# Attention stage of a two-layer encoder: new-key copy behind the exponentials, high x parts on GpSimd, and weight casts behind the x casts

## The chip, the cores and the metric

The kernel runs on one core of one Trainium2 chip. The metric is the device time of one execution in microseconds (us). Engines are named as the profile names them: PE (TensorE, matrix products; PEld is its weight load), DVE (VectorE), ACT (ScalarE), POOL (GpSimd), SP (SyncE, which only issues DMAs here).

## The reference, cut to what matters

Two layers of an encoder process 640 rows of width 1024: 512 rows of one new stream and 16 rows of each of 8 running streams. Layer 0 is feed-forward, then an S5 state space beside stick-breaking attention, then feed-forward. Layer 1 is feed-forward, Mamba-2, feed-forward. Each part ends in a layer norm of (ALPHA * x + part).

```python
def swiglu(x, w_gate, w_up, w_down):
    return (jax.nn.silu(x @ w_gate) * (x @ w_up)) @ w_down

def sb_block(q_blk, q_pos, k, v):                       # stick-breaking attention
    z = jnp.einsum('bqhd,bkhd->bhqk', q_blk, k) * (SB_HEAD_DIM ** -0.5)
    mask = k_pos[None, :] < q_pos[:, None]
    sp = jnp.where(mask, jax.nn.softplus(z), 0.0)
    suffix = lax.cumsum(sp, axis=3, reverse=True) - sp
    w = jnp.where(mask, jnp.exp(jax.nn.log_sigmoid(z) - suffix), 0.0)
    return jnp.einsum('bhqk,bkhd->bqhd', w, v)

# mixer of layer 0
g = jax.nn.gelu(ys + d_skip * u)                        # ys: S5 output
s5_out = g * jax.nn.sigmoid(g @ w_glu + b_glu)
out = concatenate([s5_out, sb_out], axis=-1) @ w_out    # w_out: 8 blocks of 128 rows
```

## The kernel before, in words

**Products in three parts.** Each fp32 operand is split in a high part, a cast to PE's reduced fp32 format (`hi`, mostly on ACT, line 95), and a low part, the difference (`lo`, DVE, line 96). A product is three matmuls: high with high, low with high, high with low. x lies transposed in `xhi` and `xlo`, 8 blocks of 128 channels by 640 rows; the rows are five tiles t = 0 to 4 of 128. A weight block is loaded by SP into one of four `raw` tiles, and split by `load_w` into one of six `w` tiles.

**Phases.** ffn0, mix0, ffn1, ffn2, mix1, ffn3 follow each other. Within a phase a list scheduler sets each engine's order, by what it takes to be ready; `tc.issue_after(i)` puts what is traced under it behind instruction i, on the engine of i alone. It sets an order, not a wait.

**Entry of an ffn.** While the layer norm of the phase before ends, `layer_norm` leaves a closure `transposes` for each row tile t: 8 transposes on PE, and a split of their PSUM banks into `xhi` and `xlo`. Those of t = 3 and 4 run within the ffn's first products: gate and up of weight blocks f = 0 and 1 on rows 0 to 255 first, then on rows 256 to 639, which need tiles 2, 3 and 4. After them come the gate products of blocks 2 and 3 (lines 278 to 286), then `down` for blocks 0 and 1, and then pairs of blocks in a form with fewer products (`operands`, `matrix`), of which `operands` for `w_up` of f = 2 is the first: its loads go through `raw`, and one of its casts is of a single 128x512 piece into a tile of its own.

**The attention stage** (lines 914 to 1404) is written out by hand: a loop over 16 units s = (p, u), p being one of four pairs of heads, u one of four pieces of work (u = 3 is the running streams). At its end the order in which the program was traced is fixed on PE, ACT and DVE (`in_order`); POOL and SP are left to the scheduler. An iteration s holds, in this order:
- `turn(s)` transposes the weights on PE into a pair of PSUM banks z, an ACT copy (line 1361) takes them out, and `product(s)` multiplies by the values on PE.
- `begin(s + 2)` makes the scores of a later unit in z, and `soft(s + 2)` runs three ACT functions on them.
- `sums(s + 2)` on DVE adds, scans and subtracts (lines 1256, 1263, 1265), reading the same z; `expo` is then ACT's exponential of that.
- For u = 1 the idle columns of z also take a transpose of the new keys; ACT's copy of it, line 1201 into `kk`, is the first of two steps that turn the keys around (`new_keys`).

Between these, `fill` places matmuls of other work on PE: query and key projections of later pairs, the sigmoid gate of the S5 output (`glu_groups`) and the first half of the output projection (`out_groups`). Its side work waits in two lists of jobs, for ACT and for DVE; `slot(engine, us)` takes ready jobs from a list until their summed costs reach `us`. The jobs are weight splits (lines 1086, 1089), x splits (`split_x`, lines 1123, 1124), sigmoids (three ACT functions on `gs`, line 83) and evictions. Blocks 0 to 3 of `w_out` are split in the loop; blocks 4 to 7 are loaded by `load_w` behind it (line 1410), where the scheduler may place their casts between the fixed instructions.

Of the kernel before, what the change touches and what calls it, by code (L numbers as in the profile page):

```python
# [9 lines left out]
F32 = mybir.dt.float32  # L10
# [26 lines left out]
def kernel(ctx: ExitStack, tc: tile.TileContext, I, O, phases=PHASES):  # L37
# [123 lines left out]
    def layer_norm(t, g_bc, last):  # L161

        y = yacc[:, t, :]
        st = small.tile([128, 2, 6], F32, name="st")
        mv = small.tile([128, 2], F32, name="mv")
        rs = small.tile([128, 1], F32, name="rs")
        for j in range(2):
            nc.vector.bn_stats(st[:, j, :], y[:, j * 512:j * 512 + 512])  # L168
        nc.vector.bn_aggr(mv, st)
        nc.vector.tensor_scalar_add(rs, mv[:, 1:2], LN_EPS / ALPHA ** 2)  # L170
        state["pow"] = nc.gpsimd.tensor_tensor(rs, rs, mhalf, op=ALU.pow).ins
        if t < NT - 1 and not last:
# [7 lines left out]
            nc.gpsimd.tensor_tensor(y[:, hi], y[:, hi], g_bc[1][:, hi], op=ALU.add)  # L180
        else:
            nc.vector.scalar_tensor_tensor(y, y, mv[:, 0:1], g_bc[0], op0=ALU.subtract, op1=ALU.mult)  # L182
            for c in [slice(0, 512), slice(512, 1024)] if last and t == NT - 1 else [slice(0, 1024)]:
                state["ln"] = nc.vector.scalar_tensor_tensor(y[:, c], y[:, c], rs, g_bc[1][:, c],  # L184
                                                             op0=ALU.mult, op1=ALU.add).ins
                if last:
                    nc.sync.dma_start(O["y"][t * 128:t * 128 + 128, c], y[:, c])
        if last:
            return
        xh, xl = xt["hi"], xt["lo"]  # L190

        def transposes():
            for j in range(2):
                pt = bank_b().rearrange("p (k c) -> p k c", c=128)
                for k in range(4):
                    nc.tensor.transpose(pt[:, k, :], y[:, (4 * j + k) * 128:(4 * j + k) * 128 + 128], ident)
                split(xh[:, 4 * j:4 * j + 4, t * 128:t * 128 + 128],
                      xl[:, 4 * j:4 * j + 4, t * 128:t * 128 + 128], pt)

        pend.append(transposes)  # L200

# [10 lines left out]
    def ffn(i, ph, last, side=None):  # L212
# [4 lines left out]
        with ExitStack() as st:  # L217
# [58 lines left out]
            first = {}  # L276
            g_row = lambda: wk.tile([128, T], F32, name="s", bufs=2)
            for r in range(2):
                w = load_w(I["w_gate"][i, 2 + r])
                first[r] = g_row()  # L280
                for c in range(2):
                    p = bank_a()[:, :Q]
# [102 lines left out]
            def pair(f, before=None):  # L385
# [26 lines left out]
                for n, take in (("w_gate", gate), ("w_up", up)):  # L412
# [2 lines left out]
                        continue  # L415
                    if n == "w_up" and before is not None:
                        down(before)
                    with tc.issue_after(state["acc0"]) if f == 2 else ExitStack():
                        A = operands(I[n][i, f], I[n][i, f + 1])
                    if n == "w_up":  # L420
                        for r in range(2):
# [307 lines left out]
    def mixer0(ph, last):  # L729
# [184 lines left out]
        with ExitStack() as st:  # L914
# [61 lines left out]
                    self.done = True  # L976
                    self.give()

            todo = {"act": [], "dve": []}
            groups = []  # L980

            def later(engine, cost, give, *needs):
# [3 lines left out]

            def slot(engine, us):

                while us > 0:
                    todo[engine] = sorted((j for j in todo[engine] if not j.done), key=lambda j: not j.frees)  # L990
                    j = next((j for j in todo[engine] if j.ready()), None)
                    if j is None:
                        return
                    j.run()
                    us -= j.cost
# [124 lines left out]

            def split_x(k, src, o, L, needs):

                a = later("act", 0.1 + 0.001 * L, lambda: nc.scalar.copy(xh[:, k, o:o + L], src[:, o:o + L]), *needs)
# [50 lines left out]
            def out_groups():  # L1174
                for t in range(NT):
                    for j in range(2):
                        def operands(t=t, j=j):
                            for k in range(4):
                                wo[k] = ws["o", k][:, 0], ws["o", k][:, 1]
                            return bank_a(), three(x_cols(range(4), 128 * t, 128), [w_j(wo[k], j) for k in range(4)])  # L1180

                        def then(ps, t=t, j=j):
                            def give():
# [171 lines left out]
            for s, (p, u) in enumerate(units):  # L1355
# [14 lines left out]
                    streams_back(p)  # L1370
                if s + 2 < len(units):
                    soft(s + 2)
                if u == 2:
                    V.tensor_copy(qk[p, "q"][:, 0:512], po[p])
                slot("dve", 3.8)
                if u == 3:
                    streams_out(p)
                    if p < 3:
# [3 lines left out]
                if u == 0:  # L1382
                    kr[p].run()
                slot("act", 1.2)
                fill(FILL[1])
                if (p, u) == (3, 2):
                    split_x(7, qk[3, "q"], 0, TP, [made[3, n, h] for n in "qk" for h in range(2)])
            while groups:
# [1 line left out]
                    slot("act", 1)  # L1390
                    slot("dve", 1)
                fill(1)
            while todo["act"] or todo["dve"]:
# [13 lines left out]
        with ExitStack() as st:  # L1407
            ctx_p.close()
            open_banks()
            for k in range(4, 8):  # L1410
                wo[k] = load_w(I["m0_out"][k])
            gb = pool("m0_gb", 1, st, reuse_waits="tile")
            g_bc = [gb.tile([128, D], F32, name=f"gb{n}") for n in range(2)]
# [561 lines left out]
```

## Time and profile before

| what | value |
|---|---|
| device time, median of 3 runs | 2573.09 us (2572.42 to 2573.87) |
| the profiled execution | 2573.02 us; its span 2571.3 us |
| PE busy, PEld busy | 2511.2 us (98%), 2297.1 us (89%) |
| DVE, ACT, POOL busy | 2017.1 us, 1225.1 us, 287.3 us |
| mean granted clock of PE | 0.992 |
| attention stage | about 572 to 736 us of the span |
| start of ffn1, ffn2, ffn3 | about 764, 1195 and 2119 us |

A timeline row has the start in us, the duration in us, the engine, the line, the operation, the tiles it writes and reads with shapes, the number of instructions merged, and in brackets the idle time of the engine before it and what ended that. In a table by stretch each engine has its busy time, then come PEclk (the share of full speed granted to PE) and the DMA share. In a group row, what stands behind the first bar is the summed time and the mean duration in ns.

### The profile page before, as it was taken

Reading aid. Unit: us, or ns where it says so; the run is one execution under the profiler, and the core shown is the slowest. Engines: PE = TensorE matmul, PEld = TensorE weight load, DVE = VectorE, ACT = ScalarE, POOL = GpSimd, SP = SyncE. Lnnn points to the kernel's source line nnn. Section 1 sums busy time; section 2 is a strip of 40 time slices with the busy share of each in tenths; the row PEclk is TensorE's granted clock in tenths of the full one; section 3 lists DMA queues with packets and bytes.
Section 4 is the critical chain, followed back from the end, with each engine's and each line's share of the span. In section 5 each row is a group of like instructions: output and inputs, shape, how many; then the busy total and the mean of one; then the engine's idle time right before and its main releaser. Section 6 shows DMA issues by size and latency. Waiting matters only on the chain. (4 is left out here: it accounts for less than half of the span.)

```text
span 2571.3 us, 40672 instructions
## 1 busy us (share of the span) xinstructions
PE 2511.2 (98%) x15577; PEld 2297.1 (89%) x15577; DVE 2017.1 (78%) x3685; ACT 1225.1 (48%) x2329; POOL 287.3 (11%) x412
## 2 busy tenths in 40 slices
PE   8999999999899999999999999999999999999998
PEld 8999999878678999998999999889989878999997
DVE  7788877666768888887888887778686798876768
ACT  4443444336743555553455554566565443443332
POOL 0000002110030000003000002311111150000001
PEclk9999999999999999999999999999999999999999
DMA  5332334443311334443144434356564722443442
GB/s 183 107 97 86 107 115 153 150 159 101 96 53 55 107 96 110 119 126 105 53 111 114 116 106 132 114 184 193 159 203 141 238 72 80 161 150 110 143 138 95
DMA packets 174835, 317.44 MB, mean 123 GB/s; under 512 B 20480, under 2 KB 91776, under 8 KB 174128
## 3 DMA queue, kind: packets, MB, share of 16 engines
q1 hardware_dynamic: 164816, 293.83, 35.7%
q0 software_dynamic: 9824, 21.01, 4.0%
q8 instruction: 122, 2.00, 0.3%
q14 instruction: 73, 0.60, 0.1%
HBM read 259.56 MB, written 40.54 MB: 117 GB/s over the span
## 5 line engine op out<-in xcount | busy, mean ns | idle before, releaser
L96 DVE TENSOR_TENSOR w<-raw,w 128x512 fp32r<-128x512 f32 (+1 forms) x601 | 525.8, 899 | 84.7 <-ACT w L95 83.6
L95 ACT CAST w<-raw 128x512 fp32r<-128x512 f32 (+1 forms) x601 | 442.3, 776 | 289.7 <-PE bank L134 106.9
L356 PE MATMUL bank<-xhi,w 128*128 128x320 f32 x2432 | 540.0, 309 | 1.0 <-ACT mx L367 0.9
L134 PE MATMUL bank<-xhi,w 128*128 128x256 f32 (+2 forms) x2272 | 502.5, 313 | 14.5 <-ACT xhi L95 8.2
L134 PE MATMUL bank<-w,h 128*128 128x512 f32 x1872 | 435.1, 390 | 0.0
L356 PE MATMUL bank<-T,w 128*128 128x320 f32 x2736 | 426.3, 309 | 0.8 <-DVE s L393 0.4
L134 PEld LDWEIGHTS bank<-w,h 128*128 128x128 f32 x1872 | 349.2, 188 | 72.5 <-DVE h L96 1.0
L356 PEld LDWEIGHTS bank<-xhi,w 128*128 128x128 f32 x2432 | 407.4, 188 | 5.0 <-ACT mx L367 1.8
L356 PEld LDWEIGHTS bank<-T,w 128*128 128x128 f32 x2736 | 406.4, 188 | 2.8 <-DVE s L393 1.2
L134 PEld LDWEIGHTS bank<-xhi,w 128*128 128x128 f32 x2272 | 382.2, 190 | 26.1 <-ACT xhi L95 9.5
L356 PE MATMUL bank<-xlo,w 128*128 128x320 f32 x1216 | 375.1, 308 | 0.0
L134 PE MATMUL bank<-xlo,w 128*128 128x256 f32 (+2 forms) x1136 | 353.8, 312 | 5.8 <-DVE xlo L96 5.8
L356 PEld LDWEIGHTS bank<-xlo,w 128*128 128x128 f32 x1216 | 228.0, 188 | 0.3
L134 PEld LDWEIGHTS bank<-xlo,w 128*128 128x128 f32 x1136 | 215.9, 190 | 7.7 <-DVE xlo L96 7.0
L209 DVE SCALAR_TENSOR_TENSOR yacc<-bank,yacc 128x512 f32<-128x512 f32 x160 | 109.4, 687 | 77.8 <-PE bank L134 77.2
L367 ACT COPY mx<-bank 128x320 f32<-128x320 f32 x228 | 96.4, 423 | 142.2 <-PE bank L356 141.7
L96 DVE TENSOR_TENSOR w<-sw,w 128x1024 fp32r<-128x1024 f32 x76 | 93.0, 1224 | 52.9 <-ACT w L95 52.6
L95 ACT CAST w<-sw 128x1024 fp32r<-128x1024 f32 x76 | 79.8, 1051 | 99.0 <-DVE sw L335 97.9
L500 POOL DMA_DIRECT2D yacc<-ev x56 | 48.6, 904 | 651.2 <-ACT ev L499 591.2
L134 PE MATMUL bank<-w,og 128*128 128x512 f32 x432 | 104.9, 396 | 3.0 <-DVE og L1769 2.8
L134 PEld LDWEIGHTS bank<-w,og 128*128 128x128 f32 x432 | 79.6, 188 | 21.0 <-DVE og L1769 4.6
L395 ACT ACTIVATE s<-s 128x320 f32<-128x320 f32 x108 | 50.8, 471 | 84.0 <-DVE s L393 83.8
(428 smaller groups left out, 3467.0 us busy)
## 6 DMA issues: line engine op xcount, KB each, us to landing
raw<-in_w_gate_dram SPq DMA_DIRECT2D x88, 512.0 KB, 3.8
raw<-in_w_up_dram SPq DMA_DIRECT2D x88, 512.0 KB, 4.0
raw<-in_w_down_dram SPq DMA_DIRECT2D x88, 512.0 KB, 3.6
raw<-in_m_in_dram SPq DMA_DIRECT2D x52, 512.0 KB, 4.6
yacc<-ev POOLq DMA_DIRECT2D x56, 256.0 KB, 4.3
raw<-in_m_out_dram SPq DMA_DIRECT2D x24, 512.0 KB, 4.1
csb<-cs_d SPq DMA_DIRECT2D x20, 512.0 KB, 4.9
h<-in_ssd_h_dram SPq DMA_DIRECT2D x16, 512.0 KB, 6.1
```

The source lines that it names most:

```text
L95: nc.scalar.copy(hi, src)
L96: return nc.vector.tensor_tensor(lo, src, hi.bitcast(F32), op=ALU.subtract)
L134: state["pe"] = nc.tensor.matmul(ps, a, b, start=(k == 0), stop=(k == n - 1)).ins
L209: state["acc"] = nc.vector.scalar_tensor_tensor(ya, pb, scale, ya, op0=ALU.mult, op1=ALU.add).ins
L356: nc.tensor.matmul(ps, A[p][:, a, k * 128:k * 128 + 128], B[p][b][:, k, :], start=(first and n == 0), stop=(n == 11), skip_group_check=True)
L367: nc.scalar.copy(e[n], ps)
L395: state["silu"] = nc.scalar.activation(t, ps, AF.Silu).ins
L500: nc.gpsimd.dma_start(yacc[:, t, 512 * j:512 * j + 512], e, accum_op=ALU.add)
```

## The change

Five edits:
1. **New keys.** The first copy into `kk` (line 1201) is traced right behind the three functions of `soft`, ahead of `sums`, for the three later pairs of heads.
2. **x casts on POOL.** A third list of jobs, for POOL, takes the high half of `split_x`: 20 casts, of 256, 384, 512 or 640 columns. A call of `slot` for ACT or DVE first gives out all POOL jobs that are ready. The low halves stay on DVE. DVE's slot in the loop is 4.6 instead of 3.8.
3. **Two weight splits in the kept order.** Blocks 4 and 5 of `w_out` are loaded and split by `load_w` in iterations 12 and 13, and so stand at fixed places; 6 and 7 stay behind the loop.
4. **ffn weights behind the last x casts.** `layer_norm` keeps its last ACT cast of x (`xc`). The loads of gate blocks 2 and 3, and `operands` for `w_up` of f = 2, are put behind it on ACT. It is there for ffn1, ffn2 and ffn3; ffn0 has none.
5. `out_groups` no longer writes its weights into `wo`, so that blocks 4 and 5 may be placed there earlier.

```diff
@@ layer_norm, transposes @@
-                split(xh[:, 4 * j:4 * j + 4, t * 128:t * 128 + 128],
-                      xl[:, 4 * j:4 * j + 4, t * 128:t * 128 + 128], pt)
+                state["xc"] = nc.scalar.copy(xh[:, 4 * j:4 * j + 4, t * 128:t * 128 + 128], pt).ins
+                nc.vector.tensor_tensor(xl[:, 4 * j:4 * j + 4, t * 128:t * 128 + 128], pt,
+                                        xh[:, 4 * j:4 * j + 4, t * 128:t * 128 + 128].bitcast(F32), op=ALU.subtract)
@@ ffn @@
             for r in range(2):
-                w = load_w(I["w_gate"][i, 2 + r])
+                with tc.issue_after(state["xc"]) if "xc" in state else ExitStack():
+                    w = load_w(I["w_gate"][i, 2 + r])
...
-                    with tc.issue_after(state["acc0"]) if f == 2 else ExitStack():
+                    with ExitStack() as q:
+                        if f == 2:
+                            for k in ("acc0", "xc"):
+                                if k in state:
+                                    q.enter_context(tc.issue_after(state[k]))
                         A = operands(I[n][i, f], I[n][i, f + 1])
@@ mixer0 @@
-            todo = {"act": [], "dve": []}
+            todo = {"act": [], "dve": [], "pool": []}
...
             def slot(engine, us):
 
+                if engine != "pool":
+                    slot("pool", 100)
...
-                a = later("act", 0.1 + 0.001 * L, lambda: nc.scalar.copy(xh[:, k, o:o + L], src[:, o:o + L]), *needs)
+                a = later("pool", 0.1 + 0.001 * L, lambda: nc.gpsimd.tensor_copy(xh[:, k, o:o + L], src[:, o:o + L]),
+                          *needs)
...
                 if s + 2 < len(units):
                     soft(s + 2)
+                    if units[s + 2][1] == 1:
+                        kr[units[s + 2][0]].needs[0].run()
...
-                slot("dve", 3.8)
+                slot("dve", 4.6)
...
                 slot("act", 1.2)
+                if s in (12, 13):
+                    wo[s - 8] = load_w(I["m0_out"][s - 8])
...
-            for k in range(4, 8):
+            for k in range(6, 8):
                 wo[k] = load_w(I["m0_out"][k])
```

The order of PE's instructions is the same before and after, throughout the program. What moves stands on ACT, DVE, POOL and SP.

**ACT in the attention stage**, from the copy of one unit's values on (`pvs`, unit 7) to the next copy of transposed weights (`es<-bank`, unit 8), with what each instruction waits for. Before:

```order
L1303 COPY pvs<-bank 128x256 [waits PE_49]
L1246 ACTIVATE es<-bank 128x2x384 [waits PE_49]
L83 ACTIVATE es<-es 128x2x384 [waits Activation_49] x2
L1201 COPY kk<-bank 128x128 [waits DVE_49]
L83 ACTIVATE gs<-gs 128x256
L83 ACTIVATE gs<-gs 128x256 [waits Activation_49] x2
L1361 COPY es<-bank 128x1024 [waits PE_49]
```

And with the change:

```order
L83 ACTIVATE es<-es 128x2x384 [waits Activation_49] x2
L1209 COPY kk<-bank 128x128
L83 ACTIVATE gs<-gs 128x256 [waits DVE_49]
L83 ACTIVATE gs<-gs 128x256 [waits Activation_49] x2
L83 ACTIVATE gs<-gs 128x256 [waits DVE_49]
L83 ACTIVATE gs<-gs 128x256 [waits Activation_49] x2
L1369 COPY es<-bank 128x1024 [waits PE_49]
```

The copy of the new keys waited for DVE and now has no wait of its own; a second sigmoid (three functions) now stands ahead of the copy of the weights.

**ACT at the entry of ffn1**, from the table load for silu on; `xhi<-bank` are the casts of x (the two singles are those of t = 4), `hf` the silu of a gate, `w_8068` the single piece of `operands` for f = 2. Before:

```order
L272 ACT_TABLE_LOAD
L272 ACTIVATE hf<-bank 128x256
L95 CAST xhi<-bank 128x4x128 x2
L95 CAST h<-hf 128x256
L272 ACTIVATE hf<-bank 128x256
L95 CAST w_8068<-raw 128x512
L95 CAST xhi<-bank 128x4x128
L95 CAST h<-hf 128x256
L95 CAST xhi<-bank 128x4x128
L272 ACTIVATE hf<-bank 128x384
```

And with the change:

```order
L273 ACTIVATE hf<-bank 128x256
L197 CAST xhi<-bank 128x4x128
L95 CAST h<-hf 128x256
L197 CAST xhi<-bank 128x4x128
L95 CAST w<-raw 128x512 x4
L273 ACTIVATE hf<-bank 128x384
L95 CAST w<-raw 128x512 x2
L95 CAST w_8068<-raw 128x512
L95 CAST w<-raw 128x512 x2
```

The single piece moves from ahead of the x casts of t = 4 to behind them, and the four casts of gate blocks 2 and 3 follow them too.

**DVE at the entry of ffn3**, from the last layer norm instruction on; `xlo<-bank` are the low parts of x, `w<-raw` those of weights. Before:

```order
L184 SCALAR_TENSOR_TENSOR yacc<-yacc,rs,h_21059 128x1024
L96 TENSOR_TENSOR w<-raw,w 128x512 x4
L273 TENSOR_TENSOR hf<-bank,hf 128x256
L96 TENSOR_TENSOR xlo<-bank,xhi 128x4x128
L96 TENSOR_TENSOR h<-hf,h 128x256
L96 TENSOR_TENSOR xlo<-bank,xhi 128x4x128
L1439 MEMSET xrow 128x512
L1440 MEMSET brow 128x256
L1457 TENSOR_TENSOR h_21861<-h_21861,el_21843 128x512
L1457 TENSOR_TENSOR h_21906<-h_21906,el_21843 128x512
L273 TENSOR_TENSOR hf<-bank,hf 128x256
L96 TENSOR_TENSOR xlo<-bank,xhi 128x4x128
```

And with the change:

```order
L184 SCALAR_TENSOR_TENSOR yacc<-yacc,rs,h_21059 128x1024
L1451 MEMSET xrow 128x512
L1452 MEMSET brow 128x256
L274 TENSOR_TENSOR hf<-bank,hf 128x256
L198 TENSOR_TENSOR xlo<-bank,xhi 128x4x128 x2
L96 TENSOR_TENSOR h<-hf,h 128x256
L274 TENSOR_TENSOR hf<-bank,hf 128x256
L198 TENSOR_TENSOR xlo<-bank,xhi 128x4x128
L96 TENSOR_TENSOR h<-hf,h 128x256
L198 TENSOR_TENSOR xlo<-bank,xhi 128x4x128
L96 TENSOR_TENSOR w<-raw,w 128x512 x4
```

The four low parts of weights move behind the low parts of x, and the two products of line 1457 (1469 now) go further back; at the same place SP now issues twelve small loads for `xrow` and `brow` ahead of the two loads for `operands` of f = 2, where it issued them behind.

More of the change, by code (lines that the diff above doesn't have):

```diff
@@ L1177, in operands @@
                         def operands(t=t, j=j):
-                            for k in range(4):
-                                wo[k] = ws["o", k][:, 0], ws["o", k][:, 1]
-                            return bank_a(), three(x_cols(range(4), 128 * t, 128), [w_j(wo[k], j) for k in range(4)])
+                            w = [(ws["o", k][:, 0], ws["o", k][:, 1]) for k in range(4)]
+                            return bank_a(), three(x_cols(range(4), 128 * t, 128), [w_j(v, j) for v in w])
                         def then(ps, t=t, j=j):
@@ L1392, in mixer0 @@
                 fill(1)
-            while todo["act"] or todo["dve"]:
+            while any(todo.values()):
                 slot("act", 1)
```

## The prediction

> **What bounds the kernel now.** I read the page's head first, then the table of PE's waits, then the timelines around its largest stops.
>
> ```profile
> span 2571.3 us, 40672 instructions
> PE 2511.2 (98%) x15577; PEld 2297.1 (89%) x15577; DVE 2017.1 (78%) x3685; ACT 1225.1 (48%) x2329; POOL 287.3 (11%) x412
> ...
> PE bank L1285 <- ACT es L1361: 12.9, 5, 4.9
> ...
> ACT kk L1201 <- DVE S L1265: 11.2, 3, 3.9
> ```
>
> PE is busy for 98% of the span and does the same products in the same order with the change. So a gain can come only from its 60.1 us of idle time (2571.3 - 2511.2), and from slow-clock stretches that follow a stop. A row of waits has the total, the number of waits and the longest. PE's row is its largest: attention products waiting for the copied weights (the stops at the entries of the feed-forward parts come below). The other row, from ACT's waits, says why the copy of weights is late: the new-keys copy ahead of it waits for DVE's sums.
>
> ```profile
> 624.31 1.09 PE L1285 MATMUL bank<-es,vt 128*64 128x128 f32 x16 [1.01 <-ACT es L1361]
> 662.47 1.97 PE L1285 MATMUL bank<-es,vt 128*64 128x128 f32 x16 [4.01 <-ACT es L1361]
> 673.66 0.88 PE L1285 MATMUL bank<-es,vt 128*64 128x128 f32 x12 [0.66 <-ACT es L1361]
> 683.39 1.55 PE L1285 MATMUL bank<-es,vt 128*64 128x128 f32 x12 [4.87 <-ACT es L1361]
> 700.78 1.03 PE L1275 MATMUL bank<-ident,S 128*128 128x128 f32 x8
> 706.00 1.58 PE L1285 MATMUL bank<-es,vt 128*64 128x128 f32 x16 [2.35 <-ACT es L1361]
> ```
>
> The bracket is the stop. A stop also costs clock behind it. In the table by stretch PEclk stands behind POOL's column:
>
> ```profile
> 624.30:628.00 3.70, 3.69 (x42) 3.36 (x43) 1.29 (x2) 3.46 (x6) 0.00 (x0) 1.00 0.41 109
> 662.50:666.00 3.50, 3.50 (x28) 2.88 (x29) 2.55 (x6) 3.44 (x7) 0.00 (x0) 0.57 0.22 35
> 683.40:689.00 5.60, 5.60 (x23) 3.38 (x24) 4.23 (x8) 4.21 (x7) 0.00 (x0) 0.50 0.05 19
> 706.00:710.00 4.00, 4.00 (x31) 3.27 (x32) 0.10 (x1) 0.95 (x2) 0.00 (x0) 0.57 0.00 0
> 784.20:789.00 4.80, 4.78 (x17) 4.78 (x17) 4.44 (x10) 0.76 (x2) 0.00 (x0) 0.56 0.00 0
> 2135.30:2144.00 8.70, 6.60 (x23) 6.28 (x24) 6.96 (x16) 1.51 (x3) 0.00 (x0) 0.61 0.39 135
> ```
>
> Behind the 1.01 us stop the clock stayed at 1.00; behind 2.35, 4.01 and 4.87 it was 0.50 to 0.57. PE's busy time times (1 - clock) is what a stop costs besides its length.
>
> **New keys, the copy (edit 1).** ACT around the longest of these waits:
>
> ```profile
> 654.46 1.73 ACT L83 ACTIVATE es<-es 128x768 f32<-128x768 f32 x2
> 660.04 0.27 ACT L1201 COPY kk<-bank 128x128 f32<-128x128 f32 x1 [3.85 <-DVE S L1265]
> 660.21 1.31 ACT L83 ACTIVATE gs<-gs 128x256 f32<-128x256 f32 x3
> 661.43 0.99 ACT L1361 COPY es<-bank 128x1024 f32<-128x1024 f32 x1
> 665.19 0.84 ACT L83 ACTIVATE S<-S 128x768 f32<-128x768 f32 x1
> 674.12 1.63 ACT L83 ACTIVATE gs<-gs 128x384 f32<-128x384 f32 x3
> 676.69 0.81 ACT L1246 ACTIVATE es<-bank 128x768 f32<-128x768 f32 x1 [0.20 <-PE bank L1237]
> 682.56 0.78 ACT L1361 COPY es<-bank 128x768 f32<-128x768 f32 x1
> ```
>
> *662.47.* PE was free at 662.47 - 4.01 = 658.46. With the change: exponentials end at 654.46 + 1.73 = 656.19, the key copy takes 0.27, two sigmoids (the order has a second one here) 2 x 1.31, and from the copy's start to PE it is 662.47 - 661.43 = 1.04. That is 660.1, so 1.7 remains and 2.3 is gained. A stop of 1.7 lies between one that kept the clock (1.01) and one that lost it (2.35); I take it as kept, which saves 3.50 x 0.43 = 1.5, with 0 as the other end.
>
> *683.39.* The product before it started at 673.66. The absolute value started 676.69 - 673.66 = 3.03 behind that; then come 0.81, the exponentials 1.73, one sigmoid 1.63 and 683.39 - 682.56 = 0.83: 8.03 against 9.73 before. Gain 1.7; a stop of 3.2 remains, and with it the slow clock (5.60 x 0.50 = 2.8, which I do not count).
>
> *706.00.* PE was free at 703.65. Its transposes end at 701.81, and 1.04 later the weights could be used, 0.8 ahead of need. The stop goes: 2.35, and 4.00 x 0.43 = 1.7 of clock. *624.31* goes too (1.0), as does 673.66 (0.6), since ACT is less loaded.
>
> Together 1.0 + 2.3 + 1.5 + 1.7 + 2.35 + 1.7 + 0.6 = 11.15.
>
> **Casts on POOL (edit 2), splits in the order (edits 3, 5).** Twenty casts leave ACT for POOL. Their price on POOL is in no row; the nearest are these, with the row of sixteen casts on ACT, and DVE's weight splits, first alone, then while POOL adds:
>
> ```profile
> L778 POOL COPY r8t<-r 128x256 f32<-128x256 f32 x4 | 1.8, 454 | 57.4 <-DVE zb L817 57.4
> ...
> L1482 POOL TENSOR_SCALAR cw<-cw 128x120 f32<-128x120 f32 x1 | 1.7, 1661 | 0.0
> ...
> 767.45 1.63 POOL L180 TENSOR_TENSOR yacc<-yacc,gb 128x512 f32<-128x512 f32 x1
> ...
> L1123 ACT CAST xhi<-g x16: 388/460/524, 632.1 to 703.9; 128x256 fp32r<-128x256 f32 x8, 128x384 fp32r<-128x384 f32 x8
> ...
> 1206.90 1.28 DVE L96 TENSOR_TENSOR w<-raw,w 128x512 fp32r<-128x512 f32 x2
> ...
> 766.73 2.90 DVE L96 TENSOR_TENSOR w<-raw,w 128x512 fp32r<-128x512 f32 x2
> ```
>
> ACT is rid of 16 x 0.46 = 7.4 us and of four longer ones, all beside PE except where it stood ahead of a copy (0.6, counted above). The row of sixteen covers 8 x 256 + 8 x 384 columns, the other four by the code 3 x 640 + 512: 7552. The copy gives 454 / 256 = 1.77 ns a column, 13.4 us in all; the two-input add 3.2 ns, 24 us; the tensor-scalar 13.8 ns, 104 us. I take the copy, the only row with one input and one output of this width. POOL had 11% to do, so even 24 us there costs nothing by itself; a cast costs only where DVE's low half behind it, in DVE's fixed order, delays the sums. The cover for that is about 5 us: the sums of the unit at 660 were ready when the key copy went (660.04), and their exponential ran at 665.19.
>
> On DVE, slot 4.6 instead of 3.8 puts up to 0.8 us more ahead of some sums, mostly another weight split of 0.64; and POOL's reading can stretch a split from 0.64 to 1.45 (half of 2.90), by 0.81. Bounds: 0 (all in the cover) to 8 (half of twenty such blocks on the path). I take 0.5, near the covered end, because of those 5 us. The Trainium skill's page "SBUF — State Buffer" (section "Who interferes with whom") states that a DVE instruction with two SBUF inputs contends with a GpSimd one that reads SBUF, and that the later is blocked completely; the row at 766.73 agrees in kind. By it every low half and scan that meets a cast would be late: the upper end.
>
> The casts of blocks 4 and 5 on ACT move to later iterations. I cost that at nothing: four casts of some 0.6 are spread over two iterations, and without ACT's idle time there they would be 1.2 each, ahead of one copy. Attention: 11.15 - 0.5 = 10.65.
>
> **Weights behind the x casts (edit 4), ffn1 and ffn2.**
>
> ```profile
> 783.07 0.62 ACT L95 CAST w<-raw 128x512 fp32r<-128x512 f32 x1 [3.35 <-DMA raw<-in_w_up_dram]
> ...
> 784.22 1.97 PE L134 MATMUL bank<-xhi,w 128*128 128x384 f32 x5 [4.73 <-ACT xhi L95]
> ...
> 1207.16 1.14 PE L134 MATMUL bank<-xhi,w 128*128 128x384 f32 x5 [0.24 <-ACT xhi L95]
> 1209.17 0.44 PE L134 MATMUL bank<-xlo,w 128*128 128x384 f32 x1 [0.87 <-DVE xlo L96]
> ```
>
> In ffn1 the single piece of the up weights waits 3.35 for its DMA, and the x casts of t = 4 stand behind it on ACT. In ffn2, where nothing stands ahead of them, the same stop is 0.24. So 4.73 - 0.24 = 4.5 goes, and the clock loss 4.78 x 0.44 = 2.1: 6.6. The piece then waits behind the x casts, with casts for gate blocks 2 and 3 around it; PE has over 8 us of products on rows 256 to 639 first, so I cost that at nothing, and at the 3.35 if that cover is gone. In ffn2 the two splits at 1206.90 stood ahead of the low part of x; behind it, the stop of 0.87 goes: 0.9.
>
> **ffn3.**
>
> ```profile
> 2131.25 2.48 DVE L96 TENSOR_TENSOR w<-raw,w 128x512 fp32r<-128x512 f32 x4
> 2133.66 0.41 DVE L273 TENSOR_TENSOR hf<-bank,hf 128x256 f32<-128x256 f32 x1
> ...
> 2135.32 1.14 PE L134 MATMUL bank<-xhi,w 128*128 128x384 f32 x5 [2.72 <-ACT xhi L95]
> 2135.65 0.48 DVE L1439 MEMSET xrow<- 128x512 f32 x1
> ...
> 2136.34 1.22 DVE L1457 TENSOR_TENSOR h<-h,el 128x512 f32<-128x512 f32 x2
> ...
> 2138.54 0.69 PE L134 MATMUL bank<-xlo,w 128*128 128x384 f32 x1 [2.08 <-DVE xlo L96]
> ```
>
> Four splits delay `hf` (2133.66), ACT's cast of h waits for it, and the x cast stands behind. With the change two memsets stand there: 0.48 and about half that. So `hf` ends near 2131.25 + 0.75 + 0.41 = 2132.4; ACT then has the three steps that took 2135.32 - 2134.07 = 1.25 from the end of `hf` to PE: near 2133.7. PE was free at 2135.32 - 2.72 = 2132.60, so 1.1 to 1.2 remains of 2.72. Of the second stop (2.08) I leave 0.4 for the low halves. Gain 1.5 + 1.7 = 3.2; two stops near 1 keep the clock, 6.60 x 0.39 = 2.6. Off go 0.5 for splits now late on DVE and for the loads of `operands` behind twelve small loads on SP: 5.3, with 2.7 (no clock) and 5.8 as ends.
>
> **Sum.** Attention 10.65, ffn1 6.6, ffn2 0.9, ffn3 5.3: 23.45. The profiled execution took 2573.02, 1.7 above its span and 0.07 below the median, so I use it as it is: 2573.02 - 23.45 = 2549.6, said as 2549.5.
>
> **Rivals.**
>
> *A, more clock.* The remaining stop near 683 does not lose the clock: 2.8 more, 2546.7. Against: a stop of 2.35 lost it at 706. The Trainium skill's page "TensorE: Matmul & The Clock Gate" (section "What's actually happening") says that the clock halves after an idle window of about 3.4 us that runs on freely; by that rule 3.2 may escape, and 2.35 should have. The row disagrees, so the rule only speaks for some luck with the window's phase.
>
> *B, POOL and DVE block each other.* 20 x 0.81 = 16.2, half on the path: 8 instead of 0.5, 2557. For: the row at 766.73. Against: the 5 us cover.
>
> *C, the entries pay half.* Another instruction (the silu, `hf`) becomes what the x casts wait for: half of 12.8, 2556. Against: ffn2's stop of 0.24 in the same order.
>
> *D, slower.* POOL casts go at the tensor-scalar's 13.8 ns a column. A batch of 4 x 384 + 640 = 2176 columns then takes 30 us, four casts of 256 take 14, and the later 2688 columns 37. DVE's low halves wait for them in order, ahead of sums; beyond 5 to 10 us of cover each, some 59 of these 81 us come on the path and the attention gain is lost: 2573.0 - 12.8 + 59 = 2619. It decides from about 8 ns a column, or 2 us for a cast of 256. Against: the copy's 454 ns.
>
> *E, the copy still waits* (on the bank or the new `kk` tile): attention gains some 2, 2558. Against: the order shows no wait on it.
>
> **Chances.** Forecast 0.48, A 0.22, B 0.15, C 0.08, D 0.04, E 0.03. About 0.2% (5.1 us) is what a measurement of this kernel can tell from no change; only D is slower (0.04), I leave 0.02 for a sum of half-failures within it, and 0.94 is faster. The forecast's own range, from the ends named (clock at 662, 0 to 2 on DVE, 2.6 at ffn3), is 2545.5 to 2553; to hold 8 in 10 with A and most of B and C it is 2543 to 2559.
>
> **What would show it.** Right: no wait of the key copy on DVE's sums; PE's stops on the weights' copy falling from 12.9 to about 5, nearly all in two stops of 1.7 and 3.2; clock 1.00 behind 662 and 706; POOL casts near 0.45 us for 256 columns; the stop in ffn1 near 0.24, and in ffn3 two of about 1. Wrong: DVE waiting for POOL's `xhi` ahead of sums, scans or splits that got longer, a new stop of PE at the gate products of blocks 2 and 3 or at the first products of pairs, or a clock that stays at 0.5 where the stop went.

## The result and the profile after

The changed kernel takes 2548.61 us (median of five runs, 2542.40 to 2551.85) against 2573.09 us before (five runs beside it, 2570.48 to 2573.91). The ratio is 0.9899, with a 95% interval of 0.9885 to 0.9913: 1.0% faster, 24.5 us. The forecast was 2549.5. The profiled execution took 2548.97 us.

From here on, lines of the changed kernel are its own: the copy into `kk` is L1209 (L1201 before), the copy of the weights L1369 (L1361), the product L1293 (L1285), the cast of x at a feed-forward part's entry L197 (L95), the cast on POOL L1131 (L1123 on ACT).

The page's head and two rows of PE's waits, after:

```profile
span 2547.3 us, 40681 instructions
...
PE 2501.8 (98%) x15577; PEld 2289.1 (90%) x15577; DVE 2017.0 (79%) x3685; ACT 1218.0 (48%) x2309; POOL 298.3 (12%) x432
...
PE bank L1293 <- ACT es L1369: 4.3, 2, 3.0
...
PE bank L134 <- ACT xhi L197: 1.8, 4, 1.1
```

The last of these rows, before:

```profile
PE bank L134 <- ACT xhi L95: 8.2, 5, 4.7
```

The span is 24.0 us shorter. PE's idle time fell from 60.1 to 45.5 us (2547.3 - 2501.8), its busy time by 9.4 us although its products are the same: that part is clock (the mean granted clock rose from 0.992 to 0.997). The two waits fell from 12.9 to 4.3 and from 8.2 to 1.8 us.

PE's remaining stops at the places of the change, from the timeline, and the granted clock (1.00 or 0.50, behind POOL's column) behind the first two, behind 694, where the stop of 2.35 us had been, and in ffn1:

```profile
658.75 1.09 PE L1293 MATMUL bank<-es,vt 128*64 128x128 f32 x16 [1.34 <-ACT es L1369]
675.05 1.55 PE L1293 MATMUL bank<-es,vt 128*64 128x128 f32 x12 [3.00 <-ACT es L1369]
768.13 1.14 PE L134 MATMUL bank<-xhi,w 128*128 128x384 f32 x5 [0.24 <-ACT xhi L197]
1189.11 1.14 PE L134 MATMUL bank<-xhi,w 128*128 128x384 f32 x5 [0.24 <-ACT xhi L197]
2115.45 1.14 PE L134 MATMUL bank<-xhi,w 128*128 128x384 f32 x5 [1.08 <-ACT xhi L197]
```

```profile
658.70:662.70 4.00, 3.95 (x39) 3.62 (x40) 3.40 (x8) 2.45 (x3) 0.81 (x2) 1.00 0.03 9
675.00:680.60 5.60, 5.55 (x23) 3.33 (x24) 5.17 (x9) 3.91 (x6) 1.54 (x2) 0.50 0.00 0
694.00:698.00 4.00, 4.00 (x38) 3.12 (x37) 3.96 (x6) 1.81 (x3) 0.00 (x0) 1.00 0.00 0
768.00:773.00 5.00, 4.87 (x28) 4.87 (x29) 4.89 (x10) 2.95 (x7) 0.00 (x0) 1.00 0.20 44
```

Of these only the stop of 3.00 us still costs clock (behind 1189 and 2115 it was 1.00 too). The second stop that ffn3 had (2.08 us), ffn2's 0.87, and the attention stops of 1.01, 0.66 and 2.35 us are gone.

ACT ahead of the product at 658.75, and at the entry of ffn1:

```profile
653.49 1.73 ACT L83 ACTIVATE es<-es 128x768 f32<-128x768 f32 x2
655.12 0.25 ACT L1209 COPY kk<-bank 128x128 f32<-128x128 f32 x1
655.27 2.52 ACT L83 ACTIVATE gs<-gs 128x256 f32<-128x256 f32 x6
657.70 0.99 ACT L1369 COPY es<-bank 128x1024 f32<-128x1024 f32 x1
...
767.50 0.59 ACT L197 CAST xhi<-bank 128x512 fp32r<-128x512 f32 x1 [2.28 <-PE bank L196]
767.98 0.41 ACT L95 CAST h<-hf 128x256 fp32r<-128x256 f32 x1
768.28 0.59 ACT L197 CAST xhi<-bank 128x512 fp32r<-128x512 f32 x1
768.76 2.19 ACT L95 CAST w<-raw 128x512 fp32r<-128x512 f32 x4
```

The `kk` copy has no bracket any more: it runs in the slot behind the exponentials, and two sigmoids (six functions, 2.52 us) now stand between it and the copy of the weights. In ffn1 the casts of x wait only for PE's own transposes, and the casts of weights stand behind them.

Measured from landmark to landmark in the two timelines, the 24.0 us split so: from the start of the attention products (584.85 before, 584.77 after) to ffn1's first product on tile 2, 16.0 us less, of which 4.5 are that product's own stop; to ffn2's, 2.0 (ffn1's clock); to ffn3's, 1.8 (the stops in ffn2 and ffn3, with some 0.7 lost between); to the end, 4.1 (most of ffn3's second stop and its clock).

### The profile page after: what moved, and what is told of

It reads as the page before. It is cut to its first block, busy times and chain, and to the rows that moved or that the text cites. A ratio compares the mean times of both kernels' runs of the same rounds, so it can differ in the third digit from the quotient of the medians.

```text
span 2547.3 us, 40681 instructions
## 1 busy us (share of the span) xinstructions
PE 2501.8 (98%) x15577; PEld 2289.1 (90%) x15577; DVE 2017.0 (79%) x3685; ACT 1218.0 (48%) x2309; POOL 298.3 (12%) x432
## 5 line engine op out<-in xcount | busy, mean ns | idle before, releaser
L95 ACT CAST w<-raw 128x512 fp32r<-128x512 f32 (+1 forms) x601 | 441.7, 776 | 286.5 <-PE bank L134 102.7
L134 PE MATMUL bank<-xhi,w 128*128 128x256 f32 (+2 forms) x2272 | 497.3, 311 | 8.2 <-ACT w L95 6.2
L95 ACT CAST w<-sw 128x1024 fp32r<-128x1024 f32 x76 | 79.9, 1051 | 98.1 <-DVE sw L337 96.9
```

Of the source, the lines that this page charges most:

```text
L95: nc.scalar.copy(hi, src)
L134: state["pe"] = nc.tensor.matmul(ps, a, b, start=(k == 0), stop=(k == n - 1)).ins
```

## The experiments

Each run was timed beside the kernel before on the same chip; between the groups of runs the chip differs, so times of different groups are best compared by their ratios. In the runs of the second and third group of four, the kernel before had medians of 2571.93 and 2573.71 us.

### The parts by themselves

**Edit 4 alone** on the kernel before:

```diff
             for r in range(2):
-                w = load_w(I["w_gate"][i, 2 + r])
+                with tc.issue_after(state["xc"]) if "xc" in state else ExitStack():
+                    w = load_w(I["w_gate"][i, 2 + r])
...
-                    with tc.issue_after(state["acc0"]) if f == 2 else ExitStack():
+                    with ExitStack() as q:
+                        if f == 2:
+                            for k in ("acc0", "xc"):
...
```

> The kernel before with edit 4 alone (weights behind the last x casts). Theory (the prediction's steps): 4.5 us of stop and 2.1 of clock in ffn1, 0.9 in ffn2, 3.2 and 2.1 in ffn3: 12.8 us, 2560.3; its stops read about 0.24 in ffn1 and 1.1 in ffn3. Rival (the gain of the whole change is mostly attention's or luck of the clock elsewhere): under 8 us, above 2565.

2560.64 us (2558.78 to 2562.66), ratio 0.9954 (0.9942 to 0.9967). Its stops at the entries of ffn1 and ffn3:

```profile
777.54 1.14 PE L134 MATMUL bank<-xhi,w 128*128 128x384 f32 x5 [0.24 <-ACT xhi L197]
2125.66 1.14 PE L134 MATMUL bank<-xhi,w 128*128 128x384 f32 x5 [0.24 <-ACT xhi L197]
```

The theory's 12.8 us is met in sum: 2573.38 (before, nine runs) less 2560.64 is 12.7. In ffn3 the stop is 0.24 and not 1.1, though the order on DVE is that of the change; so the 1.1 is the meeting of two timings, not a fixed wait. The change itself, profiled again (the control below), has 0.24 there too.

**The change without edit 4**, the same lines the other way round:

```diff
-                with tc.issue_after(state["xc"]) if "xc" in state else ExitStack():
-                    w = load_w(I["w_gate"][i, 2 + r])
+                w = load_w(I["w_gate"][i, 2 + r])
...
```

> The change without edit 4. Theory: attention gains 10.65 us, and the ffn entries stay as before (4.73 us of stop in ffn1): 2562.4. The two parts together should give the 24 us of the whole change. Rival (they overlap, or the clock's luck carries part of it): the two gains add up to less than 20 or more than 28 us.

2561.65 us (2559.28 to 2562.79), ratio 0.9957 (0.9945 to 0.9970): 11.7 us. The two parts together make 24.4 us, what the whole change gives. They don't overlap.

**Edit 1 alone** on the kernel before:

```diff
                 if s + 2 < len(units):
                     soft(s + 2)
+                    if units[s + 2][1] == 1:
+                        kr[units[s + 2][0]].needs[0].run()
```

> The kernel before with edit 1 alone (key copy behind the exponentials; x casts stay on ACT). Theory (the wait for DVE's sums was the whole of it, the casts only load ACT beside it): stops at 624, 662 and 706 go nearly (1.0, 3.6, 2.35) and two of the three slow-clock stretches (1.5, 1.7), the stop of 4.87 stays: about 10 us, 2563. Rival (the x casts on ACT keep the copies late): 6 us or less, 2567 or more.

2562.95 us (2561.79 to 2566.24), ratio 0.9965 (0.9951 to 0.9979): 10.4 us. PE's stops in the attention stage:

```profile
654.74 1.09 PE L1285 MATMUL bank<-es,vt 128*64 128x128 f32 x16 [0.74 <-ACT es L1361]
664.30 0.88 PE L1285 MATMUL bank<-es,vt 128*64 128x128 f32 x12 [1.07 <-ACT es L1361]
674.03 1.55 PE L1285 MATMUL bank<-es,vt 128*64 128x128 f32 x12 [4.87 <-ACT es L1361]
```

Moving one copy of 0.27 us carries nearly all of attention's gain. The stop of 4.87 us is untouched, as expected, and the one before it, 0.66 in the kernel before, is 1.07 here.

**The x casts back on ACT**, all else of the change kept:

```diff
-                a = later("pool", 0.1 + 0.001 * L, lambda: nc.gpsimd.tensor_copy(xh[:, k, o:o + L], src[:, o:o + L]),
-                          *needs)
+                a = later("act", 0.1 + 0.001 * L, lambda: nc.scalar.copy(xh[:, k, o:o + L], src[:, o:o + L]), *needs)
```

> The change with the high x parts back on ACT, all else kept. Theory: the stop before the product near 675 grows by about 1.4 (two casts ahead of its copy), the rest is hidden: 1 to 4 us above the change, 2550 to 2553. Rival (POOL and DVE block each other and the casts on POOL cost time): below the change by 2 us or more. Rival (the casts on ACT are what made the copies late): 6 us or more above it.

2550.74 us (2548.26 to 2551.35), ratio 0.9914 (0.9900 to 0.9927). That is some 2 us above the change, and the two intervals overlap.

```profile
652.82 1.09 PE L1292 MATMUL bank<-es,vt 128*64 128x128 f32 x16 [0.74 <-ACT es L1368]
...
670.11 1.55 PE L1292 MATMUL bank<-es,vt 128*64 128x128 f32 x12 [3.60 <-ACT es L1368]
```

With the casts on ACT the long stop is 3.60 instead of 3.00 (1.4 more was expected): two x casts, 0.69 us, stand ahead of its copy again. The earlier stop is 0.74 instead of 1.34: one sigmoid and a weight cast (0.60 us) stand there ahead of the copy, not two sigmoids. Between the two stops a third of 0.32 is left, at the place of the 0.66. Of the fall from 4.87 to 3.00 this kernel, which keeps edit 3 and DVE's longer slot, shows 1.3; POOL's casts brought the other 0.6. Edit 3's part can be read from ACT in the kernel before, where two of the four weight casts of blocks 4 and 5 stood between the exponentials and the copy of the long stop:

```profile
677.90 0.62 ACT L95 CAST w<-raw 128x512 fp32r<-128x512 f32 x1 [0.40 <-PE bank L1021]
679.17 0.60 ACT L95 CAST w<-raw 128x512 fp32r<-128x512 f32 x1
```

The other two stood ahead of the copy of the 0.66 us stop (668.61 and 670.34). In the change's profile all four run at 700 us and later. No run has edit 3 alone.

**The change without edit 1:**

```diff
                     soft(s + 2)
-                    if units[s + 2][1] == 1:
-                        kr[units[s + 2][0]].needs[0].run()
```

> The change without edit 1: the key copy is behind DVE's sums again, all else kept. Theory (edit 1 carries attention's gain): the waits of ACT for DVE's sums come back at three places, and with them the stops of 4 and 2.35 us near 655 and 695; 7 to 10 us slower than the change, 2555 to 2558. Rival (edits 2 and 3 alone would have unloaded ACT enough): within 4 us of the change.

2556.72 us (2554.78 to 2558.24), ratio 0.9933 (0.9920 to 0.9947), 8 us above the change. Of the two stops named, that of 4 us is back, at 4.91; the other is 0.91 and not 2.35. A row of ACT's waits and one of PE's stops:

```profile
ACT kk L1209 <- DVE S L1273: 12.1, 3, 4.8
```

```profile
661.37 1.98 PE L1293 MATMUL bank<-es,vt 128*64 128x128 f32 x16 [4.91 <-ACT es L1369]
```

The wait is back, and longer than before (12.1 against 11.2 us, the longest 4.8 against 3.9): DVE's slot of 4.6 puts more ahead of the sums. In the change ACT still waits for these sums, at their exponential: 11.8 us in nine waits, against 7.0 in six before. PE doesn't feel that: its wait for that exponential is one of 1.0 us in both kernels. The stop of 3.00 us is there without edit 1 as well, so its shortening from 4.87 is not edit 1's.

**Edits 1 and 4 alone** on the kernel before; against the change it reads:

```diff
-                slot("dve", 4.6)
+                slot("dve", 3.8)
...
-                if s in (12, 13):
-                    wo[s - 8] = load_w(I["m0_out"][s - 8])
...
-                a = later("pool", 0.1 + 0.001 * L, lambda: nc.gpsimd.tensor_copy(xh[:, k, o:o + L], src[:, o:o + L]),
-                          *needs)
+                a = later("act", 0.1 + 0.001 * L, lambda: nc.scalar.copy(xh[:, k, o:o + L], src[:, o:o + L]), *needs)
```

> The kernel before with edits 1 and 4 alone; x casts on ACT, blocks 4 and 5 of the output weights behind the loop, DVE's slot 3.8. Theory (edits 2, 3 and 5 are worth 1 to 2 us together): 2549 to 2551. Rival (they are worth the 4.87 us stop's shortening and its clock): 2553 or more.

2549.08 us (2547.20 to 2550.06), ratio 0.9901 (0.9887 to 0.9914). Two of the five edits give what all five give. What edits 2, 3 and 5 are worth together cannot be told from nothing by these runs. Their effect on PE's stops can be seen: PE waits 6.7 us here for the copied weights (0.74, 1.08 and 4.87) and 4.3 in the change. But this kernel's profile has one slow-clock stretch of 3.4 us where the change's first profile has three such lengths (see below), which at 1.7 us each outweighs the 2.4 us.

### POOL's price and its cover

The casts on POOL, grouped, after:

```profile
L1131 POOL CAST xhi<-g x16: 397/454/1090, 626.8 to 688.3; 128x256 fp32r<-128x256 f32 x8, 128x384 fp32r<-128x384 f32 x8
```

The columns are the least, median and greatest ns. The sixteen have a median of 454 ns, 460 on ACT before; it lies between two sizes, so they are better read apart. The eight of 256 columns took 401 ns on the mean (411 on ACT), the eight of 384 columns 678 (514 on ACT), from 0.5 us to 1.09. DVE's low parts, of before and of after:

```profile
L1124 DVE TENSOR_TENSOR xlo<-g,xhi x16: 411/482/552, 633.0 to 704.8; 128x256 fp32r<-128x256 f32 x8, 128x384 fp32r<-128x384 f32 x8
```

```profile
L1133 DVE TENSOR_TENSOR xlo<-g,xhi x16: 415/484/859, 632.0 to 696.8; 128x256 fp32r<-128x256 f32 x8, 128x384 fp32r<-128x384 f32 x8
```

The median is the same, the longest went from 552 to 859 ns, and the mean of the 384-column ones from 549 to 628.

To see from where POOL decides, every cast was done four times over:

```diff
-                a = later("pool", 0.1 + 0.001 * L, lambda: nc.gpsimd.tensor_copy(xh[:, k, o:o + L], src[:, o:o + L]),
-                          *needs)
+                def high():
+                    for _ in range(4):
+                        nc.gpsimd.tensor_copy(xh[:, k, o:o + L], src[:, o:o + L])
+
+                a = later("pool", 0.1 + 0.001 * L, high, *needs)
```

> The change with each of the twenty POOL casts done four times over. Theory (about 5 us of cover, POOL's work lies beside the rest): a batch of five casts takes some 13 us instead of 3.3, single ones 1.6 instead of 0.4; 0 to 5 us slower than the change. Rival (POOL's reads block DVE's two-input instructions): DVE's scans and low parts get longer than 0.94 and 0.64 us on average, and the time rises by 8 us or more.

2551.36 us (2548.99 to 2552.63), ratio 0.9912 (0.9897 to 0.9927); the change itself beside it had 2548.26. The attention stage in the table by stretch, first the change, then this kernel:

```profile
572.00:736.00 164.00, 156.10 (x1169) 126.69 (x1169) 115.98 (x172) 103.86 (x160) 16.43 (x30) 0.98 0.33 105
```

```profile
572.00:736.00 164.00, 154.70 (x1173) 126.58 (x1172) 122.37 (x173) 102.38 (x159) 56.28 (x92) 0.99 0.32 101
```

POOL works 40 us more. DVE's busy time (the third after the stretch's length) grows by 6.4 us, but with one instruction more in the stretch (x173 against x172); over the whole execution, where DVE has 3685 instructions in both, it grows from 2017.0 to 2021.7 us, by 4.7. Its scans of 384 columns took 1087 ns on the mean instead of 971, which is one of the signs that the rival named. The kernel takes about 3 us more, which the intervals don't tell from none, and not the rival's 8. So the two engines do hold each other up, as rival B of the prediction had it, but at four times the casts it costs DVE some 5 us and not 4 x 16; and rival D's point, 2 us for a cast of 256 columns, is nearly what this kernel has (4 x 0.4 to 0.5): no loss near its price appeared. The cover was larger than forecast.

### What remains, and the clock

**The change once more**, as a control:

> The change itself, once more, beside the others on one chip. Theory: 2546 to 2552, with the same two stops of attention (1.34 and 3.00 us), and slow-clock stretches at other places than in its first profile, if the clock behind a stop of 2 to 3 us is luck. Rival (the slow clock follows from the stop's length): slow stretches behind the same stops as in the first profile.

2548.26 us (2541.60 to 2550.21), ratio 0.9893 (0.9875 to 0.9912). The two attention stops are the same (1.33 and 3.00 us). Behind the 3.00 the clock was lost again, at 0.70 over the next 5.6 us and not at 0.50; in that the rival was right. Elsewhere it differs between profiles. Two other places that the change doesn't touch show it best: a product of the S5 part that waits 2.1 to 3.2 us for a low part near 470, and one of the Mamba part that waits 2.04 to 2.08 us ahead of ffn3. The stop and the stretch behind it, in the kernel before, in the change's first profile and in the control (there with the stretch behind the attention stop between the two):

```profile
472.11 0.69 PE L134 MATMUL bank<-xlo,w 128*128 128x384 f32 x1 [2.83 <-DVE xlo L96]
```

```profile
472.00:478.00 6.00, 5.89 (x19) 5.89 (x20) 0.65 (x2) 0.00 (x0) 0.00 (x0) 0.52 0.95 377
2113.70:2120.00 6.30, 5.92 (x32) 4.79 (x33) 5.28 (x12) 1.43 (x2) 2.33 (x4) 1.00 0.00 0
```

```profile
474.65 0.44 PE L134 MATMUL bank<-xlo,w 128*128 128x384 f32 x1 [2.89 <-DVE xlo L198]
```

```profile
474.60:480.00 5.40, 5.35 (x31) 5.35 (x32) 0.80 (x2) 1.23 (x3) 0.00 (x0) 1.00 0.98 391
2095.50:2102.00 6.50, 6.14 (x34) 5.00 (x35) 5.48 (x11) 1.65 (x2) 2.53 (x4) 1.00 0.00 0
```

```profile
2090.78 0.96 PE L134 MATMUL bank<-w,og 128*128 128x512 f32 x3 [2.07 <-DVE og L1781]
```

```profile
469.00:475.00 6.00, 5.93 (x25) 5.93 (x26) 0.61 (x2) 0.26 (x1) 0.00 (x0) 0.72 0.99 393
671.00:676.60 5.60, 5.58 (x27) 3.43 (x28) 5.05 (x9) 4.57 (x7) 1.55 (x2) 0.70 0.00 1
2090.70:2097.00 6.30, 5.90 (x19) 4.39 (x20) 5.28 (x12) 1.42 (x2) 2.32 (x4) 0.73 0.00 0
```

A stop of 2.83 us lost the clock (0.52) before, and one of 2.89 kept it (1.00) after; the stop of 2.07 kept it in both these profiles and lost it (0.73) in the control, which is the same program as the second. Over all fourteen profiles the stop of 2.04 to 2.08 us lost the clock in eight and kept it in six. So behind a stop of 2 to 2.9 us the slow clock differs from one execution to the next. Behind the attention stop of 3.00 us (2.99 in one) it was lost in every profile that has it, six of six.

The lengths of the slow stretches have an order of their own. Added up from stretches of 0.2 us in all fourteen profiles, each slow stretch comes to 3.41 or 6.83 us at half clock (0.50), within 0.01, and to no other length, leaving out the end of the program. A value such as 0.70 over 5.6 us is one of 3.4 us and the rest at 1.00. Where PE has work throughout, a stretch costs half its length, 1.7 or 3.4 us. In units of 3.41 us the profile before has ten, the change's first profile three, the control four.

**Two sigmoids moved behind the copy of the weights:**

```diff
-                slot("act", 1.2)
+                slot("act", 0 if s == 9 else 1.0 if s == 7 else 1.2)
```

> The change, with two sigmoids moved on ACT from ahead of the copy of weights to right behind it: the second one ahead of unit 8's copy, and the one ahead of unit 10's. Nothing else moves on any engine. Theory (the remaining stops are ACT's queue): 1.34 becomes about 0.1, 3.00 becomes about 1.4, and the slow clock behind it goes: 2.9 us of stop and up to 2.6 of clock, 3 to 5.5 faster than the change. Rival (the sigmoids only move the wait to the exponential of the sums and to the gates): under 1 us.

2548.70 us (2547.51 to 2551.43), ratio 0.9904 (0.9890 to 0.9917): no gain over the control. PE's stops there:

```profile
657.55 1.09 PE L1293 MATMUL bank<-es,vt 128*64 128x128 f32 x16 [0.76 <-ACT es L1369]
672.33 0.88 PE L1293 MATMUL bank<-es,vt 128*64 128x128 f32 x12 [1.48 <-ACT es L1369]
676.92 0.50 PE L1029 MATMUL bank<-w,xlo 128*128 128x512 f32 x1 [0.76 <-DVE xlo L1133]
685.68 0.44 PE L1315 MATMUL bank<-ident,pvs 128*128 128x128 f32 x2 [0.80 <-ACT pvs L1311]
```

The two stops shrank by 2.1 us, but two of 0.76 and 0.80 stand behind them that the control's timeline hasn't. The first is for a low part that stands on DVE behind sums which had waited 1.80 us for ACT's exponentials; the second is for a copy on ACT behind an exponential that had waited 2.71 us for DVE's sums. Most of the wait was moved, not removed. The clock behind the shortened stop stayed at 1.00, but this profile has as many slow stretches as the control's, four, at other places.

**And the S5 part's stop taken away too:** two small copies of DVE, which wait for a DMA and stood ahead of the last low parts of x, go behind them.

```diff
-                nc.vector.tensor_tensor(xl[:, 4 * j:4 * j + 4, t * 128:t * 128 + 128], pt,
+                state["xl"] = nc.vector.tensor_tensor(
+                    xl[:, 4 * j:4 * j + 4, t * 128:t * 128 + 128], pt,
...
-                V.tensor_copy(smp(hr, 0), h0[:, 0, jj])
-                V.tensor_copy(smp(hi, 0), h0[:, 1, jj])
+                with tc.issue_after(state["xl"]):
+                    V.tensor_copy(smp(hr, 0), h0[:, 0, jj])
+                    V.tensor_copy(smp(hi, 0), h0[:, 1, jj])
```

> As the run before, and in the S5 part two small copies of DVE that wait for a DMA, and what follows from them, stand behind the last low part of x instead of ahead of it. Theory: the stop of 2.89 us near 475 becomes about 0.8, so 2.1 us more than the run before, and up to 2.7 where the clock was lost behind it: 2540 to 2544. Rival: the copies' own consumers are on the path later in the S5 part, and nothing is gained.

2543.42 us (2542.76 to 2545.11), ratio 0.9884 (0.9869 to 0.9898).

```profile
468.59 0.44 PE L134 MATMUL bank<-xlo,w 128*128 128x384 f32 x1 [0.80 <-DVE xlo L198]
```

The stop is 0.80, as worked out. Then the S5 copies alone, with the sigmoids where the change has them:

```diff
-                slot("act", 0 if s == 9 else 1.0 if s == 7 else 1.2)
+                slot("act", 1.2)
```

> The change with the two copies of DVE in the S5 part behind the last low part of x, and the sigmoids where the change has them. Theory (the stop of 2.4 to 3.1 us near 470 and its slow clock are the whole gain of the version with both): 2.1 us of stop and about 1.5 of clock off the change, 2543 to 2546. Rival (the sigmoids' move gave it): same as the change, 2547 to 2550.

2546.57 us (2544.93 to 2547.20), ratio 0.9891 (0.9877 to 0.9904), between the theory's range and the rival's. And both moves again, the same program as two runs above:

> The version with both moves (sigmoids and the S5 copies) once more, beside the others. Theory: 2542 to 2545 again, at most 1 us from the version with the S5 copies alone.

2543.53 us (2541.82 to 2544.49), ratio 0.9879 (0.9866 to 0.9893). The version with both lies 3.0 us under the one with the S5 copies alone on the same chip, with no run in common: more than the "at most 1 us" expected. So the sigmoids' move gave nothing in one pair and 3 us in the other; how much of either is the clock's chance stays open. What speaks for a real gain is that the move shortens the 3.00 us stop, behind which the clock was lost every time, to 1.48. What can be said: in eight timed runs the version with both took 2541.82 to 2545.11 us; of the change's ten, seven took longer than that (up to 2551.85) and three lay at 2541.60 to 2543.53. Its median is 5 us lower, and its two profiles show no slow clock behind a stop. The 95% intervals of the ratios still overlap.

## Why the prediction was right, by its own steps

**New keys.** Right, with its sizes. The stop of 4.01 was to leave 1.7 and left 1.34; that of 4.87 was to leave 3.2 and left 3.00; those of 1.01, 0.66 and 2.35 were to go and went. The clock came back behind the first and the last and not behind the 3.00, as counted. What it put under the wrong head is the 1.7 us at 683.39: with edit 1 alone that stop stays at 4.87, and without edit 1 it is 3.00. The two weight casts that edit 3 moves and the two x casts that edit 2 moves made it shorter. Attention gave 11.5 us from landmark to landmark, 11.7 as a part by itself, against 10.65. The step left out one stop of 0.37 us behind the second copy of the keys, which went too. Its 0.5 for DVE was not to be seen on PE; on ACT the wait for DVE's sums at their exponential grew by 4.8 us, but PE's wait behind that stayed at 1.0.

**Casts on POOL.** The price taken (the copy's 1.77 ns a column) was 13% above the measured one for 256 columns (0.40 us, 1.56 ns), and that of the 384-column casts, which DVE held up, 678 / 384 = 1.77 ns. "0.6, since ACT is less loaded" was right about the stop of 0.66: it is 1.07 with edit 1 alone, 0.32 with the change's x casts back on ACT, and gone in the change, with or without edit 1. But the load was first of all edit 3's weight casts, whose move was costed at nothing, and the x casts second. The x casts' move brought 0.6 at the long stop and 0.3 at this one, and took 0.6 at the stop before, where a second sigmoid then stands ahead of the copy. In the time, edits 2, 3 and 5 together gave nothing that the runs can tell.

**Weights behind the x casts.** ffn1's stop fell to the 0.24 read from ffn2, and its clock loss of 2.1 measured 2.0. The piece behind the casts of x made no new stop: the cover on rows 256 to 639 held.

**ffn3.** DVE there, after:

```profile
2113.16 0.48 DVE L1451 MEMSET xrow<- 128x512 f32 x1
2113.65 0.27 DVE L1452 MEMSET brow<- 128x256 f32 x1
2113.84 0.36 DVE L274 TENSOR_TENSOR hf<-bank,hf 128x256 f32<-128x256 f32 x1
2114.12 1.27 DVE L198 TENSOR_TENSOR xlo<-bank,xhi 128x512 fp32r<-128x512 f32 x2
```

The memsets took the 0.75 that was counted, and the stop was 1.08 against 1.1 to 1.2. That the sizes agree is in part luck: in the control, the same program, the stop is 0.24. Of the second stop nothing remained instead of 0.4, and whether the 0.5 set aside for the late splits was needed the runs don't show: from ffn3's first product to the end 4.1 us were gained, where the second stop and the clock alone would give 4.7 (2.08 + 2.6).

**The rivals.** A's condition was met in no profile: the clock behind the 3.00 us stop was lost in all six that have it, for 6.83 us in the change's first profile and for 3.4 in the other five. The argument against A ("a stop of 2.35 lost it") was still too strong, since stops of that length keep it in some runs (2.24 and 2.31 us at 1.00); and the change's spread of 2541.6 to 2551.9 holds both A's figure and the forecast. B's contention is there, at a small part of its price. C, D and E did not happen (D's three parts hold 5888 of its 7552 columns, so by its own price it would have been slower still); D's price was passed nearly without loss in the run with fourfold casts.

So the sum came out within 1 us of the median, which is better than its terms deserve: they were off by up to 0.9 us each (attention 11.5 against 10.65), and the chance in the clock, 1.7 us a stretch, is larger than that.

## What to carry to other kernels

A short instruction that waits in order on a busy engine is priced by what stands behind it: find the row whose bracket names another engine, and ask what is queued behind it and whether its input was ready long before. A stop of the bounding engine is worth its length and what the clock loses behind it, so cutting a long stop short can pay more than the time cut off. And test the parts alone before keeping them all: here two of five edits gave all of the time that could be measured.

## What the runs showed of the hardware that was not expected

The granted clock behind a stop of 2 to 2.9 us is not set by the stop's length: 2.89 us kept it at 1.00 and 2.07 us lost it (0.73), in profiles of the same program. A stop of 3.00 us lost it in six profiles of six. Once lost, it was at 0.50 for 3.41 or 6.83 us, in each of the twelve profiles that lost it. In the attention stage, stops of 0.74 to 1.48 us kept it, but elsewhere in the change's first profile a stop of 1.34 us, close behind one of 0.33, lost it:

```profile
205.02 0.55 PE L694 MATMUL bank<-ident,s5big 128*128 128x128 f32 x3 [1.34 <-DVE s5big L619]
```

```profile
205.00:210.00 5.00, 4.98 (x21) 4.16 (x22) 2.85 (x7) 2.29 (x6) 0.21 (x1) 0.69 0.22 66
```

The Trainium skill's page "TensorE: Matmul & The Clock Gate" (section "What's actually happening") says that the activity window runs freely and does not start with the kernel, which agrees with a chance that differs from run to run; that it takes a whole idle window of about 3.4 us does not agree with the stops of 1.34 and 2.07 us that lost the clock.

POOL's cast of fp32 to PE's reduced format is as fast as ACT's (0.40 us against 0.39 for 256 columns at the least), when DVE leaves it alone; beside DVE's two-input instructions each stretched the other. One cast of 384 columns took 1.09 us (0.51 elsewhere) beside a scan that took 1.26 us (944 ns on the mean before).
